# A hybrid decoder layer on one core: head norms as one power with a kept row term, and a fixed order for POOL's factors, the gates' sigmoids and the inverse's transfers

## The chip, the core and the metric

The kernel runs on one core of one Trainium2 chip. The metric is the device time of one execution, in microseconds (us). The core has five engines with a queue each: PE (TensorE, the matmuls), DVE (VectorE), ACT (ScalarE), POOL (GpSimd) and SP (SyncE, which only issues transfers here). An engine takes its instructions in order; engines meet through semaphores.

## The reference

One layer on 1024 tokens of width 1024 (batch 1), float32. `h` is the normalised input, and one projection of it feeds everything:

```python
h = rms_norm(x, norm1_g)                      # row factor rsqrt(mean(x*x) + 1e-6)
proj = h @ w_in
p_rwkv, p_sb, q_mem, gate_logits = split(proj)
y_a = rwkv7_branch(p_rwkv, ...)               # 8 heads x 64, recurrence over time
y_b = stick_breaking_branch(p_sb, q_g, k_g)   # 8 heads x 64: q, k = rms_norm per head
y_m = memory_branch(q_mem, mem, ...)          # 4 heads x 128: q = rms_norm per head
gates = sigmoid(gate_logits)
x = x + sum_n(gates[n] * (y[n] @ w_branch[n])) @ w_out
x = x + conv_ffn(x, ...)                      # up, causal conv of width 3, SwiGLU, down
```

The head norms are the `rms_norm` of the stick-breaking q and k (64 numbers per head and token) and of the memory q (128).

## The kernel before, in words

Matmuls run in a split form: a float32 operand is a rounded high part and a low part, and a product is three matmuls (high·high, high·low, low·high; `mm3`). Each weight tile is loaded by SP (`load_w`, L76), ACT writes the high part (L80) and POOL the low part (L81). A projection (`proj_item`) is 8 blocks of six matmuls 512 wide; each block is one step of a stream of items, so that other work can be woven in between blocks. When an item begins, the weights of the next one are requested and split.

The input is not normalised before the projection: `rsc` (128 tokens × 8) is the row factor, and what comes out is scaled by it. For gates the factor is multiplied on DVE (L821, by `nrb`, the negative of it along the row); the sigmoid follows on ACT (L824) and the result is stored to memory `gsd` (L826). The sigmoid is requested at block 4 of the item that follows, by `close_gates`.

A head norm (`head_norm`) of an unscaled q or k needs the sum of squares per head and the row factor. ACT squares the tile (L843 for k, L872 for q, right behind the copies that empty the projection's banks); PE sums by column into a PSUM bank (`head_ss`); DVE multiplies by `rsc2` = rsc² (L766) and adds the small term (L170), POOL raises to −1/2 (L171) and multiplies by the row factor (L770 or L772). For k the factor is expanded on DVE (L335) and transposed by PE; for q it is the scale of the sigmoid that turns scores into weights (L920).

The stick-breaking attention (`sb_attn`) runs over 64 units: scores (PE, banks `g`), sigmoid (ACT, L920), a scan on DVE (L926), transposes (PE) with copies on ACT (L938), the weighted sum (PE) and its copies on ACT (L961). It is woven with the stream of projections. Behind it comes the attention over the memory (exponentials on ACT, L1143), then the recurrence (`stage2`), then branches, the output projection and the feed-forward part.

The recurrence needs the inverse of triangular blocks, made on DVE by 62 pairs of rows (`inverse`, L545 and L547), a memset of the diagonal (L549) and 16 transfers out to `td`, issued by POOL (L554) and read back by SP (L586). Its steps are taken along the stream: `pace` tenths of a step per step of the stream, 7 in the stick-breaking attention, 16 in the attention over the memory.

The order of instructions on an engine comes from a scheduler, which places each instruction when its modelled inputs are ready, earlier program text first. PE's matmuls are pinned to program order, and so are some others (`pinned`, `ordered`, both by `keep_in_program_order`, which puts an instruction behind the one written before it on its engine). Instructions that are not pinned may be placed ahead of their text. There are 4 PSUM banks of tag `mm` and 4 of tag `g`; the tag `w4` has three buffers, shared by q, k, their squares, the expanded factor and the gates.

Of the kernel before, what the change touches and what calls it, by code (L numbers as in the profile page):

```python
# [11 lines left out]
F32 = mybir.dt.float32  # L12
# [3 lines left out]
ALU = mybir.AluOpType  # L16
# [3 lines left out]
D = 1024  # L20
# [29 lines left out]
class Trunk:  # L50
# [25 lines left out]
        self.nc.sync.dma_start(raw, src)  # L76
        return raw

    def split_raw(self, raw, hi, lo):
        self.nc.scalar.activation(hi, raw, AF.Copy)  # L80
        self.nc.gpsimd.tensor_tensor(lo, raw, hi.bitcast(F32), ALU.subtract)  # L81
        return hi, lo

    def split_w(self, src):
# [3 lines left out]
        return self.split_raw(raw, hi, lo)  # L88

    def mm3(self, outs, w, x, first, last):  # L90
        for pi, (a, b) in enumerate(((0, 0), (0, 1), (1, 0))):
# [61 lines left out]
    def consts(self):  # L153
        nc = self.nc
        self.half = self.pool_c.tile([128, 16], F32, name="half")
        nc.vector.memset(self.half, -0.5)
        self.offs = self.pool_c.tile([128, 2], F32, name="offs")
        nc.vector.memset(self.offs[:, 0:1], OFF)
        nc.vector.memset(self.offs[:, 1:2], -OFF)
        self.omm = self.pool_c.tile([128, 14], F32, name="omm")  # L160
        nc.vector.tensor_scalar(self.omm, self.par("mu", 0, 14), 1.0, -1.0, ALU.mult, ALU.add)
        self.mun = self.pool_c.tile([128, 14], F32, name="mun")
        nc.vector.tensor_scalar(self.mun, self.par("mu", 0, 14), -1.0, None, ALU.mult)
        self.omka = self.pool_c.tile([128, 4], F32, name="omka")
        nc.vector.tensor_scalar(self.omka, self.par("k_a", 0, 4), -1.0, 1.0, ALU.mult, ALU.add)

# [371 lines left out]
    def inverse(self):  # L538
        nc = self.nc
        X = self.inst  # L540
        for s in range(1, 63):
            n = 63 - s
            tmp = self.t4("it")
            tv = tmp[:, : s * n].rearrange("p (j t) -> p j t", j=s)
            self.pinned(nc.vector.tensor_tensor(tv, X[:, 0:s, s : s + 1].to_broadcast([128, s, n]), X[:, s : s + 1, s + 1 : 64].to_broadcast([128, s, n]), ALU.mult))  # L545
            yield
            self.pinned(nc.vector.tensor_tensor(X[:, 0:s, s + 1 : 64], X[:, 0:s, s + 1 : 64], tv, ALU.add))  # L547
            yield
        nc.vector.memset(X.rearrange("p s t -> p (s t)")[:, 0 : 64 * 64 : 65], 1.0)  # L549
        for p in range(4):  # L550
            for h2 in range(2):
                for cc in range(2):
                    i0 = p * 32 + h2 * 16 + cc
                    nc.gpsimd.dma_start(self.td[p // 2, :, h2, :, p % 2, cc * 64 : cc * 64 + 64], X[i0 : i0 + 15 : 2])  # L554
                    yield

    def stage2(self):
# [3 lines left out]
        it = self.t4("it")  # L561
        ut = it[:, 0:512].rearrange("p (u c) -> p u c", u=8)
        U = [[ut[:, 2 * p + i] for i in range(2)] for p in range(4)]
        nc.gpsimd.memset(ut, 0.0)
        hq = [slice(0, 64), slice(64, 128)]
        heads = [(p, h2) for p in range(4) for h2 in range(2)]
        A, Y, W, S = (slice(o, o + 64) for o in range(0, 256, 64))
# [189 lines left out]
                self.mmul(pt[e * 64 : e * 64 + 64, u * 4 : u * 4 + 4], vl8[0:8, u * 64 : u * 64 + 64], self.ident[0:8, e:8:2], start=True, stop=True)  # L757
        nc.vector.tensor_copy(self.vlast, pt[:, :32])

    def head_norm(self, pst, nh, width, fold, neg=None):  # L760
        nc = self.nc
        n = 8 * nh
        t = self.small("hn", [128, 16])
        v3 = lambda x: x[:, :n].rearrange("p (j h) -> p j h", j=8)
        b3 = lambda x: x.unsqueeze(2).to_broadcast([128, 8, nh])
        nc.vector.tensor_tensor(v3(t), v3(pst), b3(self.rsc2), ALU.mult)  # L766
# [5 lines left out]
        nc.gpsimd.tensor_tensor(v3(f), v3(f), b3(self.rsc), ALU.mult)  # L772
        return f

    def proj_item(self, src, fin, hook={}):
        w = self.split_w(src)
        yield
        out = [self.ps("mm"), self.ps("mm")]
        for k in range(8):
            ks = slice(k * 128, (k + 1) * 128)  # L780
            self.mm3(out, [a[:, ks] for a in w], self.xin(k), k == 0, k == 7)
            if k == 4:
                self.close_gates()
            if k in hook:
                hook[k]()
            if k < 7:
                yield
        fin(out)
        yield
# [24 lines left out]
    def gate_item(self, b, d, hook={}, keep=None):  # L814
        nc = self.nc

        def fin(pp):
            g = self.t4()
            for h in range(2):
                nc.scalar.activation(g[:, h * 512 : (h + 1) * 512], pp[h], AF.Copy)  # L820
            nc.vector.tensor_tensor(g, g, self.nrb, ALU.mult)  # L821

            def close():
                nc.scalar.activation(g, g, AF.Sigmoid, scale=-1.0)  # L824
                if keep is None:
                    nc.scalar.dma_start(self.gsd[b, d], g)  # L826
                else:
                    keep["g", d] = g

            self.open_gates.append(close)  # L830

        return self.proj_item(self.I["w_in"][30 + b * 8 + d], fin, hook)

    def sb_qk(self, p, out):
# [4 lines left out]
        def k_fin(pp):  # L839
            kr, sq = self.t4(), self.t4()  # L840
            for h in range(2):
                nc.scalar.activation(kr[:, h * 512 : (h + 1) * 512], pp[h], AF.Copy)
            nc.scalar.activation(sq, kr, AF.Square)  # L843
            st["k"] = sq, kr

        def k_ss():
            st["ex"] = self.expand_heads(self.head_norm(self.head_ss(st["k"][0]), 2, SBD, 1.0))

        def k_bc():
            kr = st["k"][1]  # L850
# [17 lines left out]
        def q_fin(pp):  # L868
            qr, sq = self.t4(), self.t4()
            for h in range(2):  # L870
                nc.scalar.activation(qr[:, h * 512 : (h + 1) * 512], pp[h], AF.Copy)
            nc.scalar.activation(sq, qr, AF.Square)  # L872
            st["q"] = sq, qr

        def q_split(i):
            qr = st["q"][1]
            st.setdefault("S", []).append(self.t4("qk", F32R))
            S = st["S"][i]
            q, o = (lo64, hi64) if i == 0 else (hi64, lo64)
            g = self.par("sbq")[q]  # L880
            nc.scalar.activation(S[q], qr[q], AF.Copy, scale=g)
            nc.vector.scalar_tensor_tensor(S[o], qr[q], g, S[q].bitcast(F32), ALU.mult, ALU.subtract)
            if i == 1:
                out.extend((st["S"], *st["K"], st["f"]))

        def q_ss():
            nf = self.small("nf", [128, 16])
            st["f"] = self.head_norm(self.head_ss(st["q"][0]), 2, SBD, SBD ** -0.5, nf)
# [207 lines left out]
    def mem_q(self, h, out, hook):  # L1096
# [3 lines left out]
        def fin(pp):  # L1100
            sq = self.t4()
            qhi, qlo = self.t4("qk", F32R), self.t4("qk", F32R)
            for i in range(2):
                hs = slice(i * 512, (i + 1) * 512)
                self.pinned(nc.scalar.activation(qhi[:, hs], pp[i], AF.Copy, scale=self.par("memq")))
                nc.scalar.activation(sq[:, hs], pp[i], AF.Square)
                self.pinned(nc.vector.scalar_tensor_tensor(qlo[:, hs], pp[i], self.par("memq"), qhi[:, hs].bitcast(F32), ALU.mult, ALU.subtract))
            st.extend((sq, qhi, qlo))

        def ss():  # L1110
            sq, qhi, qlo = st
# [3 lines left out]
            out.extend((qhi, qlo, self.head_norm(pst, 1, 128, 128 ** -0.5)))  # L1115

        return self.proj_item(self.I["w_in"][26 + h], fin, hook), ss

# [759 lines left out]
    def run(self):  # L1878
# [27 lines left out]
        gate = lambda hook={}: self.gate_item(*gq.pop(0), hook)  # L1906
        mark = lambda name: lambda: marks.add(name)
        for p in range(4):
            kp, kss, qp, hooks = self.sb_qk(p, qk[p])
            items += [*([self.differ] if p == 0 else []), kp, gate({6: self.spread_last} if p == 0 else {}), kss, qp, gate(hooks), mark(f"sb{p}")]  # L1910
        prep, mss, mv, mk = self.mem_kv()
        mqi = [None] * 4
        for h in range(4):
# [122 lines left out]
```

## Time and profile before

| | us |
|---|---|
| median of 3 runs | 1805.65 |
| lowest and highest | 1805.49, 1806.79 |
| the profiled execution | 1808.55 |
| its span, first to last instruction | 1806.8 |

The span is what the profile accounts for; the rest of an execution's time lies around it. Busy shares of the span: PE 99%, weight loads 80%, DVE 65%, ACT 48%, POOL 44%. A matmul's record covers its way through the array, so that neighbours overlap and the end is modelled; what a wait costs is better read from the starts. In rows of waits stands: engine, tile and line, `<-` what ended the wait, then total us, times, longest. In rows of a timeline: start, length, engine, line, operation, tiles written and read, shape, count, and in brackets the idle time of the engine before it and what ended that.

### The profile page before, as it was taken

To read this page: it belongs to the slowest core of one execution; us is meant where nothing else is said; L and a number is where in the kernel's file an instruction comes from. 1 tells how busy PE (TensorE), PEld (TensorE's weight loads), DVE (VectorE), ACT (ScalarE), POOL (GpSimd) and SP (SyncE) were. 2 spreads that over 40 slices of the span, in tenths; PEclk is the share of its full clock that TensorE was granted. 3 is DMA by queue.
4 is the path that set the end of the run, shared out by engine and by line. 5 is a ranking of instruction groups with operands and counts; after the bars stand their busy time and mean duration, and the time that the engine had idled before them with its cause. 6 is when DMAs were issued, how large, how long until landed. Compare 5 with 4: busy or idle time off the path is not lost.

```text
span 1806.8 us, 27325 instructions
## 1 busy us (share of the span) xinstructions
PE 1783.4 (99%) x10479; PEld 1446.0 (80%) x10479; DVE 1182.9 (65%) x1626; ACT 864.3 (48%) x1556; POOL 791.7 (44%) x448
## 2 busy tenths in 40 slices
PE   9999999999999999999999999989999999999999
PEld 7777778888888888777777878867888888888887
DVE  5667775898987534244443872577776777795596
ACT  6444344566566535534444334543544444454343
POOL 3223353322231462122333542486767767545454
PEclk9999999999999999999999999999999999999999
DMA  5255664211112352577654553222332323486476
GB/s 208 59 163 176 196 208 157 73 42 45 53 56 88 115 129 79 192 239 277 206 187 176 186 198 106 105 87 88 123 100 88 116 101 111 134 304 226 146 237 206
DMA packets 122772, 261.29 MB, mean 145 GB/s; under 512 B 28681, under 2 KB 43657, under 8 KB 122514
## 3 DMA queue, kind: packets, MB, share of 16 engines
q1 hardware_dynamic: 85026, 193.83, 32.7%
q10 hardware_dynamic: 33840, 53.10, 8.0%
q0 software_dynamic: 3776, 12.62, 2.3%
q8 instruction: 82, 1.34, 0.3%
q14 instruction: 48, 0.39, 0.1%
HBM read 178.99 MB, written 80.48 MB: 144 GB/s over the span
## 4 chain that ended last, share of the span: by engine, by line
PE 69%; DVE 7%; ACT 3%; issue 2%; POOL 2%; DMA 1%; SPq 0%; DVEq 0%; POOLq 0%; ACTq 0%
PE mm L115 57%; PE g L115 10%; PE g L105 2%; DVE at L926 1%; DVE it L545 1%; DMA wr<-in_w_out_dram 1%; DVE mg L1294 1%; POOL wl L81 1%; DVE inst L547 1%; DMA A<-yd 0%; ACT at L1143 0%; DVE w L821 0%; DVE at L1286 0%; DVE g L1530 0%; DVE at L1287 0%
## 5 line engine op out<-in xcount | busy, mean ns | idle before, releaser
L81 POOL TENSOR_TENSOR wl<-wr,wh 128x1024 fp32r<-128x1024 f32 (+2 forms) x78 | 195.9, 2512 | 501.5 <-ACT wh L80 492.0
L115 PE MATMUL mm<-xhi,wh 128*128 128x512 f32 x784 | 260.1, 413 | 0.5 <-DVE w L322 0.4
L115 PE MATMUL mm<-xlo,wh 128*128 128x512 f32 x784 | 243.5, 392 | 0.0
L115 PE MATMUL mm<-xhi,wl 128*128 128x512 f32 x784 | 242.5, 391 | 0.0
L115 PEld LDWEIGHTS mm<-xlo,wh 128*128 128x128 f32 x784 | 147.1, 188 | 33.2 <-DVE xlo L199 0.3
L115 PEld LDWEIGHTS mm<-xhi,wl 128*128 128x128 f32 x784 | 147.0, 188 | 33.0 <-POOL wl L81 0.7
L115 PEld LDWEIGHTS mm<-xhi,wh 128*128 128x128 f32 x784 | 136.7, 190 | 29.2 <-issue 6.1
L80 ACT ACTIVATE wh<-wr 128x1024 fp32r<-128x1024 f32 (+2 forms) x78 | 81.8, 1048 | 146.4 <-PE mm L115 93.3
L115 PE MATMUL mm<-dw,da 128*128 128x512 f32 x528 | 121.0, 390 | 0.0
L115 PE MATMUL mm<-BT,wh 128*128 128x512 f32 x352 | 111.8, 399 | 6.7 <-DVE u L1585 5.8
L115 PE MATMUL mm<-BT,l 128*128 128x512 f32 x504 | 117.6, 389 | 0.0
L115 PEld LDWEIGHTS mm<-dw,da 128*128 128x128 f32 x528 | 98.9, 188 | 21.5 <-DVE da L1746 1.0
L1747 POOL TENSOR_TENSOR dw<-draw,dw 128x512 fp32r<-128x512 f32 x55 | 81.9, 1497 | 77.3 <-ACT dw L1745 75.9
L926 DVE TENSOR_TENSOR_SCAN at<-at,nrt 128x128 f32<-128x128 f32 (+3 forms) x64 | 94.2, 1479 | 25.5 <-ACT at L920 25.3
L115 PEld LDWEIGHTS mm<-BT,l 128*128 128x128 f32 x504 | 94.6, 188 | 19.7
L115 PE MATMUL mm<-B,wh 128*128 128x512 f32 x352 | 108.6, 390 | 0.0
L1746 DVE TENSOR_TENSOR da<-draw,da 128x512 fp32r<-128x512 f32 x77 | 65.9, 862 | 53.2 <-ACT da L1744 52.9
L1465 POOL TENSOR_TENSOR l<-it,l 128x1024 fp32r<-128x1024 f32 x21 | 51.2, 2436 | 92.9 <-ACT l L1462 92.8
L115 PE MATMUL g<-dw,da 128*128 128x512 f32 x396 | 90.2, 389 | 0.0
L821 DVE TENSOR_TENSOR w<-w,nrt 128x1024 f32<-128x1024 f32 x24 | 49.9, 2078 | 58.1 <-ACT w L820 47.1
L115 PEld LDWEIGHTS g<-dw,da 128*128 128x128 f32 x396 | 74.3, 188 | 15.4
L1744 ACT ACTIVATE da<-draw 128x512 fp32r<-128x512 f32 x77 | 48.1, 627 | 80.4 <-PE mm L115 32.3
(335 smaller groups left out, 3990.9 us busy)
## 6 DMA issues: line engine op xcount, KB each, us to landing
wr<-in_w_in_dram SPq DMA_DIRECT2D x48, 512.0 KB, 3.6
draw<-actd SPq DMA_DIRECT2D x77, 256.0 KB, 3.3
draw<-in_w_down_dram SPq DMA_DIRECT2D x55, 256.0 KB, 4.5
at<-scr SPq DMA_DIRECT2D x24, 512.0 KB, 5.8
wr<-in_w_up_dram SPq DMA_DIRECT2D x22, 512.0 KB, 3.5
actd<-gall ACTq DMA_DIRECT2D x44, 256.0 KB, 3.3
rw<-in_w_up_dram SPq DMA_DIRECT2D x20, 512.0 KB, 3.7
gsd<-w ACTq DMA_DIRECT2D x18, 512.0 KB, 2.8
```

What stands on the lines that cost most here:

```text
L80: self.nc.scalar.activation(hi, raw, AF.Copy)
L81: self.nc.gpsimd.tensor_tensor(lo, raw, hi.bitcast(F32), ALU.subtract)
L105: self.pinned(self.nc.tensor.transpose(out, in_, self.ident[:n, :n]))
L115: self.pinned(self.nc.tensor.matmul(*a, **k))
L545: self.pinned(nc.vector.tensor_tensor(tv, X[:, 0:s, s : s + 1].to_broadcast([128, s, n]), X[:, s : s + 1, s + 1 : 64].to_broadcast([128, s ...
L547: self.pinned(nc.vector.tensor_tensor(X[:, 0:s, s + 1 : 64], X[:, 0:s, s + 1 : 64], tv, ALU.add))
L821: nc.vector.tensor_tensor(g, g, self.nrb, ALU.mult)
L926: self.pinned(nc.vector.tensor_tensor_scan(sn[:, :W][:, ::-1], sn[:, :W][:, ::-1], self.nrt[:, 1152 - W :][:, ::-1], 1.0, ALU.mult, ALU.max))
L1465: ins = nc.gpsimd.tensor_tensor(lo, src, hi.bitcast(F32), ALU.subtract)
L1744: self.pinned(nc.scalar.activation(A[:, 0], a, AF.Copy))
L1746: self.pinned(nc.vector.tensor_tensor(A[:, 1], a, A[:, 0].bitcast(F32), ALU.subtract))
L1747: nc.gpsimd.tensor_tensor(Wt[:, 1], w, Wt[:, 0].bitcast(F32), ALU.subtract)
```

## The change

- `head_norm`: ACT copies the sums out of PSUM with a scale (1/64 or, for the memory q, 1), POOL adds a row term kept from the start (`eps`, made once from the sums of squares of the input), POOL raises to −1/2. The row factor's product is inside this one power. Its two DVE operations and POOL's final product are gone; the sign and the scale of q go into `sbn`, a scaled gain. The start makes `eps` (two small DVE operations that read PSUM) and `sbn` (one) in place of `rsc2` (one).
- The split of the next projection's weights after a head norm has its POOL part pinned behind that norm's POOL operations (`normed`, `fix`).
- Each gate's sigmoid is pinned on ACT. For items that project k of the stick-breaking heads, `close_gates` comes at block 6 in place of 4.
- The squares of q and k leave `k_fin` and `q_fin`: q's is requested at block 0 of the item behind it, k's at block 1.
- The memset of the inverse comes eight empty steps later and is pinned on DVE; `pace` in the attention over the memory is 8 in place of 16. POOL's clear of the recurrence's state (`ut`) is pinned.
- The low part of the memory q (DVE) is no longer pinned.

```diff
-    def split_raw(self, raw, hi, lo):
+    def split_raw(self, raw, hi, lo, fix=lambda ins: ins):
         self.nc.scalar.activation(hi, raw, AF.Copy)
-        self.nc.gpsimd.tensor_tensor(lo, raw, hi.bitcast(F32), ALU.subtract)
+        fix(self.nc.gpsimd.tensor_tensor(lo, raw, hi.bitcast(F32), ALU.subtract))
...
+        self.normed = False
+        self.sbn = self.pool_c.tile([128, 1], F32, name="sbn")
+        nc.vector.tensor_scalar(self.sbn, self.par("sbq"), -(SBD ** -0.5), None, ALU.mult)
...
-        self.rsc2 = self.pool_c.tile([128, 8], F32, name="rsc2")
-        nc.vector.tensor_tensor(self.rsc2, self.rsc, self.rsc, ALU.mult)
+        self.eps = self.pool_c.tile([128, 2, 8], F32, name="eps")
+        for i, n in enumerate((1.0, 128.0)):
+            nc.vector.tensor_scalar(self.eps[:, i], pst[:, :8], n * 1e-6 / D, n * 1e-12, ALU.mult, ALU.add)
...
-        nc.vector.memset(X.rearrange("p s t -> p (s t)")[:, 0 : 64 * 64 : 65], 1.0)
+        for _ in range(8):
+            yield
+        self.ordered(nc.vector.memset(X.rearrange("p s t -> p (s t)")[:, 0 : 64 * 64 : 65], 1.0))
...
-        nc.gpsimd.memset(ut, 0.0)
+        self.ordered(nc.gpsimd.memset(ut, 0.0))
...
-    def head_norm(self, pst, nh, width, fold, neg=None):
+    def head_norm(self, pst, nh, scale, eps, tag=("hf", 4)):
         nc = self.nc
         n = 8 * nh
         t = self.small("hn", [128, 16])
         v3 = lambda x: x[:, :n].rearrange("p (j h) -> p j h", j=8)
-        b3 = lambda x: x.unsqueeze(2).to_broadcast([128, 8, nh])
-        nc.vector.tensor_tensor(v3(t), v3(pst), b3(self.rsc2), ALU.mult)
-        f = self.small("hf", [128, 16], bufs=4)
-        self.rsqrt(f[:, :n], t[:, :n], n, 1.0 / (width * fold * fold), 1e-6 / (fold * fold))
-        if neg is not None:
-            nc.gpsimd.tensor_tensor(v3(neg), v3(f), b3(self.rscn), ALU.mult)
-            return neg
-        nc.gpsimd.tensor_tensor(v3(f), v3(f), b3(self.rsc), ALU.mult)
+        nc.scalar.activation(t[:, :n], pst[:, :n], AF.Copy, scale=scale)
+        nc.gpsimd.tensor_tensor(v3(t), v3(t), eps.unsqueeze(2).to_broadcast([128, 8, nh]), ALU.add)
+        f = self.small(tag[0], [128, 16], bufs=tag[1])
+        nc.gpsimd.tensor_tensor(f[:, :n], t[:, :n], self.half[:, :n], ALU.pow)
+        self.normed = True
         return f
 
-    def proj_item(self, src, fin, hook={}):
-        w = self.split_w(src)
+    def proj_item(self, src, fin, hook={}, close=4):
+        w = self.split_w(src, self.ordered if self.normed else lambda ins: ins)
+        self.normed = False
...
-            if k == 4:
+            if k == close:
                 self.close_gates()
...
-                nc.scalar.activation(g, g, AF.Sigmoid, scale=-1.0)
+                self.ordered(nc.scalar.activation(g, g, AF.Sigmoid, scale=-1.0))
...
-            nc.scalar.activation(sq, kr, AF.Square)
...
-            nc.scalar.activation(sq, qr, AF.Square)
             st["q"] = sq, qr
+
+        def square(name):
+            nc.scalar.activation(*st[name], AF.Square)
...
-        hooks = {1: lambda: k_split(1), 3: q_ss, 4: lambda: q_split(0), 6: lambda: q_split(1)}
+        hooks = {0: lambda: square("q"), 1: lambda: k_split(1), 3: q_ss, 4: lambda: q_split(0), 6: lambda: q_split(1)}
         kq = {4: k_bc, 5: lambda: k_split(0)}
-        return self.proj_item(w[18 + p], k_fin), k_ss, self.proj_item(w[14 + p], q_fin, kq), hooks
+        return self.proj_item(w[18 + p], k_fin, close=6), k_ss, self.proj_item(w[14 + p], q_fin, kq), {1: lambda: square("k")}, hooks
...
-                self.pinned(nc.vector.scalar_tensor_tensor(qlo[:, hs], pp[i], self.par("memq"), qhi[:, hs].bitcast(F32), ALU.mult, ALU.subtract))
+                nc.vector.scalar_tensor_tensor(qlo[:, hs], pp[i], self.par("memq"), qhi[:, hs].bitcast(F32), ALU.mult, ALU.subtract)
...
-        pace[0] = 16
+        pace[0] = 8
         self.weave(self.mem_attn(mq, need), pump, 1.6, 0)
```

More of the change, by code (lines that the diff above doesn't have):

```diff
@@ L87, in split_w @@
         lo = self.pool_wt.tile([128, 1024], F32R, name=self.nm("wl"), tag="wl", bufs=2)
-        return self.split_raw(raw, hi, lo)
+        return self.split_raw(raw, hi, lo, fix)
     def mm3(self, outs, w, x, first, last):
@@ L879, in q_split @@
             q, o = (lo64, hi64) if i == 0 else (hi64, lo64)
-            g = self.par("sbq")[q]
+            g = self.sbn[q]
             nc.scalar.activation(S[q], qr[q], AF.Copy, scale=g)
@@ L886, in q_ss @@
         def q_ss():
-            nf = self.small("nf", [128, 16])
-            st["f"] = self.head_norm(self.head_ss(st["q"][0]), 2, SBD, SBD ** -0.5, nf)
+            st["f"] = self.head_norm(self.head_ss(st["q"][0]), 2, 1.0 / SBD, self.eps[:, 0], ("nf", 2))
         w = self.I["w_in"]
-        hooks = {1: lambda: k_split(1), 3: q_ss, 4: lambda: q_split(0), 6: lambda: q_split(1)}
+        hooks = {0: lambda: square("q"), 1: lambda: k_split(1), 3: q_ss, 4: lambda: q_split(0), 6: lambda: q_split(1)}
         kq = {4: k_bc, 5: lambda: k_split(0)}
-        return self.proj_item(w[18 + p], k_fin), k_ss, self.proj_item(w[14 + p], q_fin, kq), hooks
+        return self.proj_item(w[18 + p], k_fin, close=6), k_ss, self.proj_item(w[14 + p], q_fin, kq), {1: lambda: square("k")}, hooks
     def sb_attn(self, qk, need):
@@ L1114, in ss @@
                 self.colsum(pst[:, j : j + 1], sq[:, j * 128 : (j + 1) * 128], self.ones[:, 0:1])
-            out.extend((qhi, qlo, self.head_norm(pst, 1, 128, 128 ** -0.5)))
+            out.extend((qhi, qlo, self.head_norm(pst, 1, 1.0, self.eps[:, 1])))
         return self.proj_item(self.I["w_in"][26 + h], fin, hook), ss
@@ L1908, in run @@
         for p in range(4):
-            kp, kss, qp, hooks = self.sb_qk(p, qk[p])
-            items += [*([self.differ] if p == 0 else []), kp, gate({6: self.spread_last} if p == 0 else {}), kss, qp, gate(hooks), mark(f"sb{p}")]
+            kp, kss, qp, early, hooks = self.sb_qk(p, qk[p])
+            items += [*([self.differ] if p == 0 else []), kp, gate({**early, 6: self.spread_last} if p == 0 else early), kss, qp, gate(hooks), mark(f"sb{p}")]
         prep, mss, mv, mk = self.mem_kv()
```

4 lines of the change are left out of this document (2 added, 2 removed).

## The prediction

> **What bounds the kernel now.** I read the page's first part, then busy time by stretches, then TensorE's waits where the changed code runs, then the timelines around each wait.
>
> ```profile
> span 1806.8 us, 27325 instructions
> PE 1783.4 (99%) x10479; PEld 1446.0 (80%) x10479; DVE 1182.9 (65%) x1626; ACT 864.3 (48%) x1556; POOL 791.7 (44%) x448
> ```
>
> PE does the same matmuls in the same order after the change: they are kept in program order and the diff adds and removes none. So the change is worth what PE's idle time is worth where the changed code runs, from 280 us (the first K projection) to about 760 us, and nothing that another engine saves counts by itself.
>
> ```profile
> 280.00:620.00 340.00, 336.04 (x2331) 279.88 (x2330) 284.11 (x265) 203.03 (x369) 97.97 (x41) 1.00 0.21 67
> 620.00:630.00 10.00, 7.72 (x69) 7.29 (x69) 0.14 (x1) 3.92 (x8) 7.41 (x5) 0.83 0.67 205
> ```
>
> Columns: stretch, length, busy PE, weight loads, DVE, ACT, POOL, granted clock. PE idles 3.96 us in the first stretch and 2.28 us in the second, where its clock is also down. The waits of 280 to 760 us are few enough to name:
>
> ```profile
> PE mm L115 <- POOL wl L81: 2.3, 1, 2.3
> PE g L115 <- ACT at L920: 2.2, 3, 1.0
> PE g L115 <- DVE hn L766: 0.9, 1, 0.9
> PE g L105 <- DVE hn L766: 0.4, 1, 0.4
> PE g L105 <- ACT at L938: 0.2, 1, 0.2
> PE g L105 <- DVE w L335: 0.2, 1, 0.2
> ```
>
> (total us, times, longest). Idle is counted from a matmul's modelled end, so it understates each wait:
>
> ```profile
> 620.99 0.28 PE L115 MATMUL mm<-qk,wl 128*128 128x256 f32 x1
> 621.11 0.40 PE L115 MATMUL mm<-qk,wh 128*128 128x256 f32 x2
> 623.79 0.39 PE L115 MATMUL mm<-qk,wl 128*128 128x256 f32 x1 [2.28 <-POOL wl L81]
> ```
>
> One such matmul follows another after 0.12 us (620.99 to 621.11). The third was due at 621.11 + 0.24 = 621.35 and came at 623.79: 2.44 us lost against 2.28 shown, so 0.16 belongs to every wait. The eight waits are 6.2 + 8 × 0.16 = 7.5 us. The longest has a tail:
>
> ```profile
> 624.90:627.90 3.00, 3.00 (x17) 2.78 (x16) 0.00 (x0) 0.09 (x1) 1.93 (x2) 0.51 0.72 194
> 627.90:631.40 3.50, 3.50 (x54) 3.33 (x53) 0.00 (x0) 1.61 (x3) 2.35 (x1) 0.93 0.58 188
> ```
>
> Behind it the granted clock is 0.51 for 3.0 us and 0.93 for 3.5 us: 3.0 × 0.49 + 3.5 × 0.07 = 1.7 us more. The whole prize is 7.5 + 1.7 = 9.2 us, 0.5% of the span. The Trainium skill, "TensorE: Matmul & The Clock Gate", in its rules, has the clock fall only after gaps over about 3 us; here 2.44 us was enough. By the page the prize would end at 7.5 us; I keep the rows' 9.2.
>
> **The inverse's transfers (pace 8, eight empty steps, ordered memset).**
>
> ```profile
> 615.02 2.40 POOL L81 TENSOR_TENSOR wl<-wr,wh 128x1024 fp32r<-128x1024 f32 x1 [3.96 <-ACT wh L80]
> 620.44 0.91 POOL L554 DMA_DIRECT2D td<-inst  x1 [3.02 <-DVE inst L547]
> 621.38 4.68 POOL L81 TENSOR_TENSOR wl<-wr,wh 128x1024 fp32r<-128x1024 f32 x2
> ```
>
> ```profile
> 616.77 1.05 ACT L80 ACTIVATE wh<-wr 128x1024 fp32r<-128x1024 f32 x1
> ```
>
> The 2.44 us wait is for the low half of a memory-K weight. ACT had its high half at 616.77 + 1.05 = 617.82 and POOL was free at 617.42, but POOL's queue holds the first transfer of the inverse (L554) ahead of it, and that one waits 3.02 us for DVE's last row (L547). Without the transfer the low half is done at 617.82 + 2.40 = 620.2, 1.1 us ahead of the 621.35 at which PE wants it. Eight empty steps at 0.7 per filler step put the transfers 11 filler steps later; of the 15 that separate this place from the attention over the memory, that leaves about four, in the last memory Q projection, where a low half has a whole projection of slack. So 2.44 + 1.7 = 4.1 us go. The next low half (ACT after 621.95) is wanted only behind the rest of this item and 3.5 us of attention matmuls (the 52 small ones in the second clock row above).
>
> What this delays: the other transfers come at 0.8 per filler step, 15 of them over 19 steps, two projections.
>
> ```profile
> L554 POOL DMA_DIRECT2D td<-inst x16: 798/810/1328, 620.4 to 663.4; - x16
> L586 SPq DMA_DIRECT2D qk<-td x16: 325/330/584, 698.6 to 935.9; - x16
> ```
>
> Their first reader is issued at 698.6, the last of them now at 663.4; two projections past the memory K (about 650 us; 48 matmuls of 0.23 us each, 11 us) is some 675 us. 23 us of cover, and SP's queue (weights, states) stays free of the wait: cost nothing. If it slipped past 699, SP would hold the weights behind it.
>
> **Squares one block on.**
>
> ```profile
> 449.16 1.06 ACT L80 ACTIVATE wh<-wr 128x1024 fp32r<-128x1024 f32 x1
> 450.12 1.04 ACT L872 ACTIVATE w<-w 128x1024 f32<-128x1024 f32 x1
> 451.07 0.93 ACT L920 ACTIVATE at<-g,nf 128x512 f32<-128x512 f32 x2
> ```
>
> ```profile
> 450.13 0.63 PE L115 MATMUL g<-qk,qk 128*128 128x512 f32 x2
> 451.79 0.39 PE L115 MATMUL g<-qk,qk 128*128 128x256 f32 x1 [1.03 <-ACT at L920]
> ```
>
> The Q square stands before the sigmoids that free the score banks. It takes ACT 451.07 − 450.12 = 0.95 us. The same happens at 527:
>
> ```profile
> 527.19 0.39 PE L115 MATMUL g<-qk,qk 128*128 128x256 f32 x1 [0.98 <-ACT at L920]
> ```
>
> Two waits of 1.03 + 0.16 and 0.98 + 0.16 each lose up to 0.95: 1.9 us. The third L920 wait (2.2 − 1.03 − 0.98, about 0.2) is not behind a square: I leave it. The moved square has two blocks (12 matmuls of 0.23) before its column sums at block 3. K's square moves too; no PE wait lies there: 0.
>
> **Head norms off DVE.**
>
> ```profile
> 383.46 0.62 PE L115 MATMUL mm<-xhi,wl 128*128 128x512 f32 x2
> 383.91 0.61 PE L115 MATMUL g<-qk,qk 128*128 128x512 f32 x2
> 385.41 0.73 PE L115 MATMUL g<-qk,qk 128*128 128x512 f32 x2 [0.88 <-DVE hn L766]
> ```
>
> ```profile
> 536.10 0.98 ACT L961 ACTIVATE ys<-mm,jk 64x128 f32<-64x128 f32 x3
> ```
>
> ```profile
> L170 DVE TENSOR_SCALAR rs<-hn x17: 167/175/2064, 296.9 to 994.0; 128x16 f32<-128x16 f32 x12, 128x8 f32<-128x8 f32 x5
> ```
>
> ```profile
> L426 ACT ACTIVATE pc<-qk x4: 227/228/231, 59.7 to 226.9; 128x16 f32<-128x16 f32 x4
> ```
>
> ```profile
> L772 POOL TENSOR_TENSOR hf<-hf,rsc x8: 203/218/222, 302.8 to 721.1; 128x16 f32<-128x16 f32 x4, 128x8 f32<-128x8 f32 x4
> ```
>
> Each of 12 norms loses two DVE operations (L766 and L170, 0.17 each, 4 us of DVE in all, worth nothing alone) and gains one ACT copy of 16 columns (0.23 from L426); POOL has a power and one small operation before and after (0.22), and the startup trades one small DVE operation for three, off PE's path while POOL forms the row factor. What counts is the PSUM bank of column sums, freed by ACT now. At 385.41 PE lost 385.41 − 383.91 − 0.45 = 1.05 us to DVE's lateness while ACT was idle: 1.0 gained. At 536.75 it lost 0.37 + 0.16 = 0.5, but there ACT itself is busy until 536.10 + 0.98 = 537.08: between +0.5 and −0.5, taken as 0. The expansion (L335) starts sooner because the power no longer follows a weight split: 0.2 + 0.16, 0.4 gained.
>
> The new load is what I can't see: 12 bank reads that now queue on ACT. Bounds per read: −0.1 (some free banks sooner) to the longest wait for ACT in the rows, 1.03 + 0.16 = 1.2. ACT is busy 203 of 340 us here, and most of its neighbours show no PE wait, so I take 0.17, 2 us in all.
>
> The ordered weight split stands behind the K norm's power. POOL does it up to 4 us later than now (the power's 3.6):
>
> ```profile
> L171 POOL TENSOR_TENSOR hf<-rs,half 128x16 f32<-128x16 f32 x12 | 43.0, 3586 | 52.5 <-DVE rs L170 42.7 <-DMA qk<-vd 9.4
> ```
>
> It is wanted a projection later, 11 us; SP's next weight load into the same buffer moves by the same 4 us inside the same slack. Nothing.
>
> **Sigmoids in order.**
>
> ```profile
> 582.63 1.07 ACT L824 ACTIVATE w<-w 128x1024 f32<-128x1024 f32 x1 [2.48 <-DVE w L821]
> ```
>
> Here ACT sat 2.48 us before a gate's sigmoid with the copies L938 queued behind it, PE's wait of 0.2 + 0.16. Held to block 4 (6 for K), the sigmoid comes when DVE is done: 0.4 gained. Its tile is stored later, but the following evacuation takes another buffer first. Past 760 us only ten or so sigmoids and the ordered clear of the recurrence's state are touched, where PE is rarely idle; taken as 0, between −1 and +1 by the waits of 0.2 to 0.4 above.
>
> **Sum.** 4.1 + 1.9 + 1.0 + 0.4 + 0.4 = 7.8 us gained, 2.0 lost again: 5.8. The profiled execution took 1808.55 us (span 1806.8, 1.75 around it), 2.9 above the median of 1805.65; I take the difference off the median: 1799.8. A measurement of this kernel tells about 0.2%, 3.6 us, from no change.
>
> **Rivals.**
> 1. The large wait stays. The low half gains only 1.1 us of margin; if ACT's split or another small POOL operation slips by more, PE still waits and the clock may still fall. For it: the scheduler orders POOL by modelled times, which put L554 too early already. Against: 1.1 us is more than any of the new small operations. Gain 7.8 − 4.1 − 2.0 = 1.7: 1804.0, no measurable change.
> 2. ACT becomes what PE waits for. If each of the 12 bank reads costs 1.2 us (the longest such wait), 14.4 − 7.8 gives +6.6: 1812.2. It decides from (7.8 + 3.6)/12 = 0.95 us per read on. For it: in the attention over the memory ACT stands in queue behind exponentials that wait for DVE,
>
> ```profile
> ACT at L1143 <- DVE nb L1140: 18.9, 6, 5.2
> ```
>
> up to 5.2 us at once, with four norms there and few banks. Against: only four of twelve lie there.
> 3. The order does nothing of the kind: squares and sigmoids find their old places, and only the norms and the transfers act. 4.1 + 1.4 − 2.0: 1802.1, on the line.
>
> The Trainium skill, "GPSIMD Engine Reference", section "Key points", says that POOL shares SBUF interfaces with DVE and contends with two-input DVE instructions. The rows agree (L545 of 236 elements took 2.6 us beside the split at 615.02, its equal L547 0.40):
>
> ```profile
> 615.07 2.60 DVE L545 TENSOR_TENSOR it<-inst 128x236 f32<-128x236 f32 x1
> 617.71 0.40 DVE L547 TENSOR_TENSOR inst<-inst,it 128x236 f32<-128x236 f32 x1
> ```
>
> This is why DVE was late for L554.
>
> **Numbers.** Forecast 0.52, rival 1 0.20, rival 3 0.15, rival 2 0.13. Forecast's own range is 1796.4 (all 9.2 us, nothing lost) to 1802. Faster: 0.52 and two thirds of rival 3, 0.62; same: rival 1, the rest of 3 and a little of 2, 0.27; slower 0.11. Range: 1796.4 to 1805.5, which leaves out rival 2 and little else.
>
> **What would show it.** After: no PE wait on POOL near 621 and clock 1.00 from 620 to 630; no wait on L766's successor at 385; L920 waits under 0.3 us near 451 and 527; transfers of the inverse after 640; sigmoids without long waits for DVE. Wrong if PE's idle time from 280 to 760 us is not down by 4 us or more, or if it has grown behind ACT, or if the stage after 760 us has moved by more than 1.

## The result, and the profile after

The changed kernel is slower: 1818.93 us median (1817.04 to 1820.28) against 1805.94 (1804.41 to 1808.66) in the same job, ratio 1.0072, 95% interval 1.0061 to 1.0082. Forecast were 1799.8, at most 1805.5. The profiled execution took 1817.41 us.

The profile's first part of the changed kernel:

```profile
span 1815.6 us, 27345 instructions
PE 1791.2 (99%) x10479; PEld 1443.5 (80%) x10479; DVE 1182.5 (65%) x1604; ACT 863.3 (48%) x1566; POOL 791.6 (44%) x448
```

PE executes the same 10479 matmuls in the same order, so the two traces can be laid on each other matmul by matmul. By the start of the same matmul, the changed kernel is 0.4 us ahead at 537 us, 4.8 ahead at 623, 3.3 behind at 735, 5.2 at 1000, 3.1 at 1250, 9.4 at 1600 and 8.8 at the end (the medians are 13.0 apart; the profiled execution of before is 2.6 above its median and the changed kernel's 1.5 below, so sizes are taken from the experiments). Three things have to be explained: the gain, a jump near 730, and a drift in a part of the kernel that the diff hardly touches.

The gain is where the prediction put it. TensorE's waits of the changed kernel, 280 to 760 us (total us, times, longest):

```profile
PE g L115 <- ACT at L1162: 5.4, 1, 5.4
PE g L115 <- ACT at L924: 1.9, 2, 1.1
PE g L105 <- DVE w L339: 1.1, 1, 1.1
PE g L115 <- ACT at L1147: 0.4, 1, 0.4
PE mm L115 <- DVE qk L1111: 0.3, 1, 0.3
```

The 2.3 us wait for POOL and the two for DVE's head norms (L766) are gone. Busy time by stretches of the changed kernel (PE, weight loads, DVE, ACT, POOL, clock):

```profile
620.00:630.00 10.00, 10.00 (x112) 9.70 (x111) 1.28 (x5) 5.43 (x11) 4.75 (x2) 1.00 0.68 241
725.00:735.00 10.00, 4.56 (x20) 3.92 (x19) 4.29 (x10) 5.97 (x16) 2.34 (x1) 0.69 0.24 79
```

The clock is 1.00 from 620 to 630, and no PE time is lost there. The jump is in the second row: PE is busy for 4.56 of 10 us and the clock falls to 0.69 (row L1162 of the waits). Its timelines in the changed kernel, PE first:

```profile
725.61 0.61 PE L115 MATMUL mm<-xhi,wl 128*128 128x512 f32 x2
731.66 1.65 PE L115 MATMUL g<-A,qk 128*128 128x256 f32 x6 [5.44 <-ACT at L1162]
```

```profile
718.81 1.41 DVE L1141 TENSOR_REDUCE mxt<-g 128x2 f32<-128x512 f32 x2 [4.67 <-PE g L115]
727.87 2.50 DVE L825 TENSOR_TENSOR w<-w,nrt 128x1024 f32<-128x1024 f32 x1 [7.65 <-ACT w L824]
730.28 0.22 DVE L1144 SCALAR_TENSOR_TENSOR nb<-mxt,hf 128x2 f32<-128x2 f32 x2
```

```profile
725.80 1.06 ACT L80 ACTIVATE wh<-wr 128x1024 fp32r<-128x1024 f32 x1 [2.58 <-PE mm L115]
726.77 1.06 ACT L824 ACTIVATE w<-mm 128x512 f32<-128x512 f32 x2
730.47 0.56 ACT L1147 ACTIVATE at<-g,nb,hf 128x256 f32<-128x256 f32 x1 [2.63 <-DVE nb L1144]
```

The softmax bias `nb` (L1144) has its maxima at 718.81 + 1.41 = 720.2, but DVE's queue holds a gate's multiply (L825) ahead of it, which waits 7.65 us for ACT's evacuation. The bias runs at 730.28, the exponentials behind it (L1147), between them the copies that free the transposes' banks (L1162), and PE stands still for 5.4 us. In the kernel before the multiply comes one unit later. From 640 to 760 us the changed kernel loses 8.7 us against the kernel before: this matmul comes 5.6 us late, the two short waits (L1147 and L1111) take 1.0, and the clock of 0.50 from 731.66 to 735.0 and 0.72 for 1.0 us more takes 1.9.

The drift has no wait. It is in the matmuls' pitch, the time from one start to the next. First the kernel before, then the changed one, both near 1400 us:

```profile
1399.77 2.66 PE L115 MATMUL mm<-B,l 128*128 128x512 f32 x11
1402.26 0.61 PE L115 MATMUL mm<-B,wh 128*128 128x512 f32 x2
```

```profile
1399.90 0.63 PE L115 MATMUL mm<-BT,wh 128*128 128x512 f32 x2
...
1402.70 0.63 PE L115 MATMUL mm<-BT,wh 128*128 128x512 f32 x2
```

Before, 11 matmuls in 1402.26 − 1399.77 = 2.49 us, 226 ns each; after, 12 in 1402.70 − 1399.90 = 2.80 us (four groups of `wh` x2 and `wl` x1), 233 ns each, at clock 1.00. The same pairs of tiles say the same: between 1225 and 1600 us `BT` with `wh` has a mean of 226.9 ns before and 233.8 after, `B` with `l` 227.2 and 233.7. By stretch, the kernel before and the changed one:

```profile
1300.00:1500.00 200.00, 200.00 (x884) 165.53 (x883) 147.98 (x222) 94.02 (x128) 148.62 (x86) 1.00 0.32 107
1650.00:1750.00 100.00, 100.00 (x442) 82.79 (x442) 61.08 (x75) 43.23 (x76) 48.69 (x36) 1.00 0.53 166
```

```profile
1300.00:1500.00 200.00, 200.00 (x868) 162.21 (x867) 147.74 (x218) 90.63 (x122) 142.98 (x83) 1.00 0.30 99
1650.00:1750.00 100.00, 100.00 (x443) 82.79 (x442) 57.64 (x70) 43.68 (x78) 49.81 (x36) 1.00 0.51 162
```

In the same 200 us of a fully busy PE at full clock, 868 matmuls in place of 884; in the down phase (1650) no difference. Summed over all start-to-start intervals that are under 0.42 us in both, PE needs 11.6 us more between 760 and 1600. The longer intervals of 1000 to 1250 us shrink by 5.8 in turn, but only 2.4 of this are shorter waits (9.4 us in all before, 7.0 after). The rest is the granted clock, the third number from the end in these rows of before and after:

```profile
1190.00:1230.00 40.00, 34.24 (x132) 27.21 (x131) 28.82 (x42) 17.14 (x24) 32.78 (x21) 0.87 0.36 111
```

```profile
1190.00:1230.00 40.00, 34.63 (x141) 27.42 (x142) 28.69 (x42) 16.57 (x23) 37.10 (x23) 0.96 0.30 99
```

That is 40 × 0.09 = 3.6 us, and the layout does not set it: e5 and e6 below have the same short pitch, and 0.91 and 0.96 there. So the two profiles by themselves make the drift look smaller than it is.

Which matmuls? The program's table of tiles, which the traces do not hold, answers. The new constants (`eps` and `sbn` in place of `rsc2`) take 64 bytes more per partition, and everything allotted behind them from the left moves by 64: the input tiles (`xhi`, `xlo`), the weights (`wr`, `wh`, `wl`), and the `l`, `B` and some of the `BT` tiles that later live there. What is allotted from the right end (`at`, `qk`, `A`, the feed-forward pool) stays. The traces agree, pair by pair. With both operands from the right (`da` and `dw`) the usual pitch is 227 ns before and after, with both from the left (`xhi` and `wl`) too. With the moving operand from the right and the stationary one from the left it goes from 227.6 to 233.2 (`at` and `wl`) and from 227.4 to 233.9 (`qk` and `mg`). Between 1225 and 1620 us, 950 of 1625 intervals between 512-wide matmuls are 233 or 234 ns, against 1 of 1619 before.

### The profile page after: what moved, and what is told of

It is laid out like the page before. It is cut to its first block, busy times and chain, and to the rows that moved or that the text cites. A ratio compares the mean times of both kernels' runs of the same rounds, so it can differ in the third digit from the quotient of the medians.

```text
span 1815.6 us, 27345 instructions
## 1 busy us (share of the span) xinstructions
PE 1791.2 (99%) x10479; PEld 1443.5 (80%) x10479; DVE 1182.5 (65%) x1604; ACT 863.3 (48%) x1566; POOL 791.6 (44%) x448
## 4 chain that ended last, share of the span: by engine, by line
PE 53%; DVE 3%; DMA 1%; POOL 1%; ACT 1%; issue 1%; DVEq 0%; SPq 0%; POOLq 0%; ACTq 0%
PE mm L115 44%; PE g L115 8%; PE g L105 1%; DMA A<-yd 1%; DVE at L1291 0%; DVE mg L1298 0%; DVE at L1290 0%; POOL wl L81 0%; DVE g L1534 0%; DMA wr<-in_w_br_dram 0%; DVE g L1535 0%; DMA wr<-in_w_out_dram 0%; DMA x<-in_x_dram 0%; DVE gall L1552 0%; POOL qk L81 0%
## 5 line engine op out<-in xcount | busy, mean ns | idle before, releaser
L81 POOL TENSOR_TENSOR wl<-wr,wh 128x1024 fp32r<-128x1024 f32 (+2 forms) x78 | 196.4, 2518 | 475.4 <-ACT wh L80 460.2
L825 DVE TENSOR_TENSOR w<-w,nrt 128x1024 f32<-128x1024 f32 x24 | 51.9, 2161 | 67.1 <-ACT w L824 56.2
```

The costliest lines, as they stand in the source:

```text
L81: fix(self.nc.gpsimd.tensor_tensor(lo, raw, hi.bitcast(F32), ALU.subtract))
```

## Experiments

All times are medians against runs of the kernel before on the same chip. "Padding" is `pad_c`, an unused tile ahead of the constants; it is 8 columns (32 bytes) wide in both kernels.

**e1 to e4: the padding, and the pace.**

```diff
-        self.pool_c.tile([128, 8], F32, name="pad_c")
+        self.pool_c.tile([128, 24], F32, name="pad_c")     # e1, e4 (on the changed kernel), e2 (on the kernel before)
...
-        self.pool_a.tile([128, 56], F32, name="pad_a")
+        self.pool_a.tile([128, 72], F32, name="pad_a")     # e3, on the changed kernel
...
-        pace[0] = 8
+        pace[0] = 16                                       # e4
```

> The changed kernel with 64 bytes more of padding ahead of its constants, so that every tile behind them stands again where it stood before modulo 128 bytes; all else, the order on each engine too, is that of the changed kernel. Theory A (half-line: a 512-wide matmul whose moving operand and stationary operand lie in different halves of a 128-byte line takes 233.3 ns from start to start, not 226.7): the pitch in the output projection and the up phase falls from 233.3 to 226.7 ns, the 11 us that TensorE needs more behind 760 us go, some 5.8 of them were covered by waits, so the time falls by 5 to 6 us to about 1813. The 5.8 us stall at 731 us stays. Rival (order: the late drift comes from the new order of ACT, POOL and VectorE work): no change, 1818.9, pitch 233.3.

1818.59 us, ratio 1.0071 (1.006 to 1.0083): no change where 1813 was expected, and the pitch stays at 233 ns. My theory of halves of 128 bytes falls here, though the rival does not follow from it, as the next run shows.

> The kernel before with 64 bytes more of padding ahead of its constants and nothing else: its small tiles, weights and left-hand operands move by 64 bytes, the right-hand operands (attention tiles, the feed-forward pool) do not. Theory A (half-line): pitch of the mixed matmuls 226.7 to 233.3 ns, 11 us more of matmul behind 760 us, some 5 to 6 of them absorbed by waits: 1805.9 to 1811 (1809 to 1815), with no stall at 731 us. Rival (order): 1805.9, no change.

1815.06 us, 1.005 (1.0037 to 1.0062). The kernel before loses 9.0 us by 64 bytes of unused memory, with every engine's order unchanged. So the drift is the layout's.

> The changed kernel with 64 bytes more of padding in the pool at the right-hand end, so that the right-hand operands too are moved by 64 bytes: now both operands of nearly every matmul lie 64 bytes past a 128-byte line. Theory A in its form 'the two operands must lie in the same half': as with the left-hand operands moved back, 5 to 6 us less than the changed kernel, about 1813, pitch 226.7 ns. Theory A in the form 'each operand must begin at a 128-byte line': no gain, 1819 or more, pitch 233 ns or above. Rival (order): no change, 1818.9.

1817.33 us, 1.0064 (1.0052 to 1.0076), 233 ns: no gain here either. Stretch 1300 to 1500 of e1, then of e3:

```profile
1300.00:1500.00 200.00, 200.00 (x869) 162.76 (x868) 147.82 (x218) 90.65 (x122) 142.02 (x82) 1.00 0.30 100
```

```profile
1300.00:1500.00 200.00, 200.00 (x869) 162.78 (x868) 147.90 (x218) 90.34 (x122) 143.79 (x83) 1.00 0.30 99
```

By the table of tiles, in e1 the left tiles begin 128 bytes past a multiple of 256 and the right ones at 0; in e3 the left at 64 and the right at 192, because padding at the right end pushes tiles down. The two displacements are equal, 128 bytes, and both are slow: a period of 128 is ruled out, and 256 is the next to try.

> The changed kernel with the padding as in the first run and with the pump's pace in the memory attention set back from 8 to 16 (the inverse's transfers are taken up more slowly there). Theory B (head of line: with pace 8 the planner puts VectorE's gate multiply of 2.5 us, which waits for ACT until 727.9 us, ahead of the 0.15 us bias of the softmax that is ready at 720.2; ACT's exponentials and TensorE's transposes then wait, 5.8 us of stall and 1.5 to 2.5 us at half clock): the stall near 731 goes, another 7 to 8.5 us less than with the padding alone: about 1805 (1800.5 to 1806), below or at the kernel before. Rival (ACT's bank reads by the twelve new copies of the head norms stall the memory attention): the stall stays, same time as with the padding alone, about 1813.

1809.51 us, 1.0015 (1.0005 to 1.0026). This is above the expected range, which counted on the padding's gain that e1 does not show; the step itself, 9.1 us less than e1 by the pace alone, is a little more than the 7 to 8.5 expected. No PE wait is left between 640 and 760. The new copies on ACT are still there, so they are not what stalled.

**e5 to e8: the period, and both repairs.**

```diff
-        self.pool_c.tile([128, 8], F32, name="pad_c")
+        self.pool_c.tile([128, 56], F32, name="pad_c")     # e5, e7, on the changed kernel
+        self.pool_c.tile([128, 16], F32, name="pad_c")     # e8, on the kernel before
...
-        self.pool_a.tile([128, 56], F32, name="pad_a")
+        self.pool_a.tile([128, 40], F32, name="pad_a")     # e6, on the changed kernel
...
-        pace[0] = 8
+        pace[0] = 16                                       # e7
```

> The changed kernel with 192 bytes more of padding ahead of its constants: with the 64 bytes that the change added, all left-hand tiles stand 256 bytes from where the kernel before has them, so moving and stationary operand have the same place in a line of 256 bytes again. Engine orders as in the changed kernel. The first four runs left this: a displacement of 64 or of 128 bytes between the two operands costs 6.6 ns for each 512-wide matmul. Theory A256 (only the difference modulo 256 bytes counts): pitch 226.7 ns everywhere behind 1225 us, time about 9 us below the changed kernel, as the kernel before lost 9.0 us by its 64 bytes: 1810 (1808 to 1812). Rival A-exact (a longer period, or the absolute place): pitch 233.3 ns, 1818.9. The stall at 731 us stays in both.

1809.29 us, 1.0015 (1.0006 to 1.0024), pitch 226.7 ns, as theory A256 says. Rival A-exact falls.

> The changed kernel with 64 bytes less of padding in the pool at the right-hand end: the right-hand operands follow the left-hand ones, all of them begin 64 bytes behind a multiple of 256. Theory A256 (the two operands of a matmul must agree modulo 256, wherever they lie): as the run before, about 1810, pitch 226.7 ns. Rival A-abs (both must begin at a multiple of 256 bytes): pitch 233 ns or above, 1818 or more.

1808.78 us, 1.0011 (1.0003 to 1.002), 226.7 ns with all operands 64 bytes past a multiple of 256 by the table of tiles. Where both operands agree, a place at 0 or at 64 makes no difference.

> The changed kernel with both repairs: 192 bytes more of padding, and the pace in the memory attention set back from 8 to 16. If theories A256 and B are both right and independent, their 9 us add up: 1818.9 less 9 less 9.1 = 1800.8 (1799 to 1803), under the kernel before by 3 to 6 us, near the 1799.8 forecast for the change without these two. If the late waits swallow what the padding gives: 1805 to 1809.

1800.26 us, 0.9962 (0.995 to 0.9974): the repairs add up. What is left of the change is worth 6.5 us (interval 4.7 to 9.0), where 5.8 was forecast; how much of that agreement is luck is said below.

> The kernel before with 32 bytes more of padding ahead of its constants, nothing else. Theory A256 with a grain of 64 bytes or coarser (the operands' places counted in steps of 64): no change, 1806. With a grain of 32 bytes or finer: the mixed matmuls at 233 ns and +9 us, 1815, as with 64 bytes. A cost that grows with the displacement would give about half, 1810.

1816.93 us, 1.0052 (1.0038 to 1.0065): 32 bytes cost 10.2 us, as much as 64 or 128 within the intervals. It is a step, not a slope. Stretch 1300 to 1500 of e5, e6 and e8:

```profile
1300.00:1500.00 200.00, 200.00 (x884) 165.72 (x883) 148.23 (x220) 94.11 (x128) 147.89 (x86) 1.00 0.32 105
```

```profile
1300.00:1500.00 200.00, 200.00 (x884) 165.62 (x883) 148.20 (x221) 94.05 (x129) 147.91 (x87) 1.00 0.32 106
```

```profile
1300.00:1500.00 200.00, 200.00 (x867) 162.51 (x866) 146.97 (x215) 90.24 (x122) 144.50 (x84) 1.00 0.31 102
```

**e9: one instruction moved** (on e5, pace 8 kept):

```diff
-            nc.vector.tensor_tensor(g, g, self.nrb, ALU.mult)
+            self.ordered(nc.vector.tensor_tensor(g, g, self.nrb, ALU.mult))
```

> The changed kernel with the padding of 192 bytes (1809.3) and its pace of 8, and one thing more: VectorE's gate multiply is kept in program order, which moves one instruction of the whole program, the multiply of 2.5 us ahead of the softmax bias near 728 us, to behind that bias; TensorE, ACT, POOL and SP have the same order. Theory B (head of line on VectorE): the stall of 5.4 us near 731 and the half clock behind it go, 1809.3 less 8 to 9 = 1800.3 to 1801.3. Rival B2 (pace 8 hurts by its transfers on POOL or the DMA queues, and the order is only a sign of it): 1809.

1805.38 us, 0.9996 (0.9988 to 1.0005): 3.4 of the 9 us by the two ratios, 3.9 by the medians of the two jobs. A miss: neither theory B's 1801 nor B2's 1809. The bias now runs at 720.35, but half of the wait is still there, and e9's ACT timeline says why:

```profile
PE g L115 <- ACT at L1162: 2.7, 1, 2.7
```

```profile
726.02 1.06 ACT L80 ACTIVATE wh<-wr 128x1024 fp32r<-128x1024 f32 x1 [2.58 <-PE mm L115]
726.99 1.06 ACT L824 ACTIVATE w<-mm 128x512 f32<-128x512 f32 x2
727.94 0.57 ACT L1147 ACTIVATE at<-g,nb,hf 128x256 f32<-128x256 f32 x1
```

ACT's order has the same fault: exponentials whose bias is there at about 720.5 stand behind a weight split and an evacuation that wait for PE. So theory B was too narrow: the scheduler had put the unit late on both engines. VectorE's part is shown by this edit; ACT's part is read from the timeline, and no run moved it at pace 8. For what e9 gained, rival B2 is out, since the transfers are those of e5. For the rest no run separates the transfers from the order, because the pace moves both; but no PE wait between 640 and 760 us names a transfer or a weight, in the changed kernel or in e9.

**e10 to e12: parts taken out of e7.**

```diff
-        w = self.split_w(src, self.ordered if self.normed else lambda ins: ins)
+        w = self.split_w(src)                                        # e10
...
+            nc.scalar.activation(sq, kr, AF.Square)                  # e11, in k_fin; q's likewise,
+            nc.scalar.activation(sq, qr, AF.Square)                  # and square() is not called
...
-                self.ordered(nc.scalar.activation(g, g, AF.Sigmoid, scale=-1.0))
+                nc.scalar.activation(g, g, AF.Sigmoid, scale=-1.0)   # e12
```

> The version with both repairs (1800.3), less the part that fixes POOL's order: the low half of a weight (2.4 us on POOL) is no longer held behind the head norm's power, and the planner puts it ahead of it for the four k blocks; nothing else moves. Theory C (the held subtraction is released at the same instant as VectorE's expansion of the head norms, runs beside it, and stretches it from 0.69 to 2.88 us in all four blocks): the expansions take 0.69 us again, the wait of 1.1 us at 304 us goes, and with VectorE 2.2 us less behind the waits at 447 and 523 us (0.8 and 1.1) shrink: 1 to 2.7 us less, 1797.6 to 1799.3. Rival C2 (the power now starts 1 to 2.4 us later, which costs as much as the stretch): no change, 1800.3, or up to 1 more.

1798.02 us, 0.9955 (0.9942 to 0.9967), the fastest of all. The expansions of the k norms, in the kernel before, in the changed one and in e10 (minimum, median and maximum ns):

```profile
L335 DVE COPY w<-hf x4: 693/694/695, 303.0 to 509.8; 128x1024 f32<-128x1024 f32 x4
```

```profile
L339 DVE COPY w<-hf x4: 2880/2890/2895, 302.1 to 508.7; 128x1024 f32<-128x1024 f32 x4
```

```profile
L339 DVE COPY w<-hf x4: 694/694/697, 302.9 to 508.1; 128x1024 f32<-128x1024 f32 x4
```

POOL, then DVE in e7, where the subtraction is still held:

```profile
298.90 3.09 POOL L774 TENSOR_TENSOR hf<-hn,half 128x16 f32<-128x16 f32 x1
301.97 2.37 POOL L81 TENSOR_TENSOR wl<-wr,wh 128x1024 fp32r<-128x1024 f32 x1
```

```profile
302.02 2.88 DVE L339 COPY w<-hf 128x1024 f32<-128x1024 f32 x1 [2.83 <-POOL hf L774]
```

The power's end frees both at once, POOL's L81 is first by 0.05 us, and the copy takes 2.37 + 0.51. In e10 L81 runs ahead of the norm, and nothing but these four instructions has moved in any engine's order; the waits at 304, 447 and 523 us shrink, and between 300 and 523 us e10 gains 2.3 us on e7.

> The version with both repairs (1800.3) with ACT's squares back at their old places, right behind the evacuations. The forecast's step on the squares: the waits for ACT near 451 and 527 us come back, 1.9 us more, 1802.2. Rival (the squares only moved those waits to 447 and 523 us, where 0.8 and 1.1 us now stand): no change, 1800.3 within 0.7.

1802.49 us, 0.9978 (0.9968 to 0.9987). TensorE's waits in e11:

```profile
PE g L115 <- ACT at L926: 4.0, 4, 1.1
PE g L105 <- DVE w L339: 1.1, 1, 1.1
```

Against 1.9 in 2 (this wait's line is L924 in the others): two waits of 1.04 come back, at 452 and 529, beside those at 447 and 524. The squares' step holds. The rival, that they only moved the waits, does not: the waits at 447 and 524 us stay when the squares go back.

> The version with both repairs (1800.3) with the gates' sigmoids no longer kept in program order. The forecast's step on the sigmoids: the wait near 584 us comes back, 0.4 to 0.5 us more, 1800.7. Rival (planner and fixed order come out alike): no change.

1800.28 us, 0.9971 (0.9959 to 0.9982). A delay of 0.39 us from start to start is back at 583 (0.50 in place of 0.11); the time cannot show so little.

**e13 and e14: the transfers alone, on the kernel before** (old norms, old layout; e14 leaves the pace at 16):

```diff
+        for _ in range(8):
+            yield
-        nc.vector.memset(X.rearrange("p s t -> p (s t)")[:, 0 : 64 * 64 : 65], 1.0)
+        self.ordered(nc.vector.memset(X.rearrange("p s t -> p (s t)")[:, 0 : 64 * 64 : 65], 1.0))
...
+        self.ordered(nc.gpsimd.memset(ut, 0.0))
...
-        pace[0] = 16
+        pace[0] = 8
```

> The kernel before with the part on the inverse's transfers alone: eight empty steps, the two fills in program order, pace 8; old head norms, old layout, so no displaced operands. Theory B (the transfers at pace 8 alone make the planner put the softmax bias and the exponentials behind the gate's evacuation): the wait at 623.8 goes with its half clock, 4.1 us gained, and the stall near 731 comes, 7 to 9 us lost: 1806.1 + 3 to 5 = 1809 to 1811. Rival (the new head norms' longer way over ACT and POOL makes the factor late): no stall near 731, 1802.

1819.10 us, 1.0075 (1.0062 to 1.0089), worse than expected: two stalls stand in the memory attention.

```profile
PE g L115 <- ACT at L1160: 8.2, 1, 8.2
PE mm L115 <- DVE qk L1109: 3.2, 1, 3.2
```

The larger one is the changed kernel's (its line is L1162 there), 2.7 us longer. Between the gate's evacuation and the exponentials e13's ACT has one thing more, the gate's sigmoid, which is not pinned here, with a load of a function table on either side:

```profile
733.38 1.28 ACT L826 ACT_TABLE_LOAD   x1
735.92 1.06 ACT L826 ACTIVATE w<-w 128x1024 f32<-128x1024 f32 x1 [1.26 <-DVE w L823]
737.42 1.28 ACT L1145 ACT_TABLE_LOAD   x1 [0.44 <-ACT w L826]
738.72 0.56 ACT L1145 ACTIVATE at<-g,nb,hf 128x256 f32<-128x256 f32 x1
```

> As the run before, with the pace left at 16. Theory B: the wait at 623.8 goes and nothing comes in its place: 1806.1 less 4.1 = 1802 (1801 to 1803). Rival: the same number, so that the two runs agree at 1802. If the eight empty steps alone already bring the stall: 1809 to 1811 for both.

1803.48 us, 0.9983 (0.9975 to 0.9992). So the transfers' part at pace 8 makes the stall without the new norms, and at pace 16 the eight steps and the two fills in order take the old wait away. Laid on the kernel before, e14 is 4.1 us ahead at 640 us, as forecast; the medians give 2.5.

## Why the prediction was wrong, point by point

The change is the sum of a gain of about 6 us, near the forecast, and two losses of 9 to 10 us each, one costed at nothing, one not looked at. In parts of the time before: after 1.0072, without the displacement 1.0015 (e5), without the pace too 0.9962 (e7).

1. **The new tiles** (in "Head norms off DVE": the startup "trades one small DVE operation for three, off PE's path"). Failed: 0.57%, 10 us (9.0 in e2). I counted the instructions and not the memory. The bound "wrong if the stage after 760 us has moved by more than 1" is what showed it: that stage takes 5.2 us more in the profiles.
2. **The inverse's transfers.** The gain is right: no wait near 621, clock 1.00, transfers from 650.6 on, and alone at pace 16 it gives 2.5 us (e14; 4.1 forecast, within its interval of 1.4 to 4.5, and 4.1 by its trace). "What this delays … cost nothing" failed, by 9 us. I let them end near 675, counting 0.23 us per projection matmul and nothing of the attention woven between. The transfers in the changed kernel, then in e7:

```profile
L560 POOL DMA_DIRECT2D td<-inst x16: 796/802/891, 650.6 to 710.1; - x16
```

```profile
L560 POOL DMA_DIRECT2D td<-inst x16: 796/796/1014, 650.8 to 676.6; - x16
```

   They end at 710.1, past the 699 that the prediction itself named as the limit. But SP's weights were not what it cost, since no PE wait there names one: the scheduler's order in the memory attention was. That the pace brings the stall is shown (e4, e7, e13 against e14), VectorE's part of it too (e9); ACT's part is read from timelines. The prediction's sign "if it has grown behind ACT" also came: PE's waits from 280 to 760 us went from 6.2 to 9.1 us. By what model time the scheduler puts the unit late no run shows; that stays open.
3. **Squares.** Right: 1.9 forecast; taken back, waits of 1.04 and 1.05 stand where e7 has 0.12 and 0.11, 1.9 us, and 2.2 in the time against e12, which lacks only the sigmoids' pin, in the same job. In the changed kernel's rows it is hard to see, since point 5 opens waits of the same kind 4 us earlier.
4. **Head norms off DVE.** Right at 385; at 536 the 0.5 taken as 0 was gained. The 2.0 for ACT's bank reads was too much: no PE wait names the new copy (L771). The new small operation on POOL was taken at 0.22 us and takes 0.19 to 1.18 (L772); no wait shows a cost of it.
5. **The expansion and the held split** ("0.4 gained", "Nothing"). Failed. The expansion does start sooner, at 302.1 in place of 303.0, but takes 2.88 us in place of 0.69: at 304 us the row of waits has 1.1 in place of 0.2, and VectorE's lateness of 4 × 2.2 us makes the waits at 447 and 523; 2.3 us in the time (e10 against e12 in one job, which also differ by the sigmoids' 0.4). The prediction quotes this very contention for L545, and did not ask what the moved L81 would now run beside. The Trainium skill, "SBUF — State Buffer", section "SBUF: two separate sides", has an exclusive lock on the ports that GpSimd shares with a VectorE instruction that uses both of its ports or has two inputs in SBUF: who starts first keeps it for the whole instruction. The rows agree: 2.88 us is L81's 2.37 and then the copy's work. That this copy uses both ports no run here shows.
6. **Sigmoids.** Right, 0.4, seen only in the trace (e12).

That the rest of the change comes near 5.8 is in part luck. By the starts in e7 up to 640 us, the old waits that went are worth 7.7 us (7.8 forecast), the three that point 5 opened cost 2.7. The forecast had taken off 2.0, for bank reads that cost nothing: a loss that did not come stood in for one that was not looked at. Without it e10 is 8.1 us below the kernel before.

Of the rivals, the first and third did not come. The second named the right place, exponentials in the memory attention behind DVE, and the wrong cause: the reads cost nothing there (e4).

## What to carry to other kernels

A new constant of a few bytes moves every tile allotted behind it: compare the address of each matmul's two operands, modulo 256 here, before and after, and give the bytes back in a padding tile. When a knob changes the pace of filler work, read its last landing and the order on every engine in the stage it ends in, not only the wait it was meant to remove. And an instruction held "behind X" starts with all else that waits for X: look at what it will run beside.

## What the hardware showed that was not expected

A 512-wide matmul whose operands begin at the same place modulo 256 bytes takes 226.7 ns; with the stationary one (from the left) 32, 64 or 128 bytes past the moving one (from the right end), about 233.3, 2.9% more, at clock 1.00 (e1 to e3, e5, e6, e8). Agreement at 0 and at 64 is equally fast; other displacements were not tried. Why a displacement costs, no run shows.
